# A four-layer trunk on one core: another order at the beginning, and the log/exp table loaded explicitly after the lower bounds

## The chip, the cores and the metric

The kernel runs on 1 core of one Trainium2 chip. The metric is the time of one execution in device microseconds. The kernel before took 3142.55 us, the median of 3 runs (3138.03 to 3144.14).

## The reference, cut to what matters

Four layers (HGRN2, RWKV-7, MLA, HGRN2) work on 256 context tokens and 256 latent tokens of 1024 channels. Each layer begins with a norm that is shifted and scaled by a modulation made from `c` and `c_ctx`. Only the beginning and the first HGRN2 layer matter here:

```python
silu_c = jax.nn.silu(c); silu_cc = jax.nn.silu(c_ctx)
mod_l = jnp.split((silu_c @ w_mod[layer] + b_mod[layer])[:, None, :], 6, axis=-1)
h_l = modulate(rmsnorm(x_l, norm1[layer]), mod_l[0], mod_l[1])
# lower bounds, from hg_lb alone
lb_p = jnp.cumsum(jax.nn.softmax(hg_lb, axis=1), axis=1); lower_bounds = lb_p - lb_p[:, :1]
# hgrn2_mixer, 8 heads of 128
q, i, g, z_f, z_b = jnp.split(h @ w_in, 5, axis=-1)
gates = jnp.log(lb + (1.0 - lb) * jax.nn.sigmoid(z)), (1.0 - lb) * jax.nn.sigmoid(-z)
b = jnp.cumsum(gc, axis=-2)     # per chunk of 64; then exp(b), exp(b - b_mid), exp(b_end - b)
o = rmsnorm(o, g_norm) * jax.nn.silu(g) @ w_o
```

## The kernel before, in words

All 512 tokens (256 of the context, 256 latent) lie transposed in SBUF, as eight tiles `xT` of 128 channels by 512 tokens. A product in float32 is made of three matmuls of split operands (`hh`/`hl` and `whi`/`wlo`): a weight tile `wraw` is cast on ScalarE (`whi`, line 432), its rest is taken on VectorE (`wlo`, 433), and both have three buffers.

`start` (342) is the beginning, called by `hgrn` for layer 0 (750). `load_x` (330) loads `x` and `ctx` through SyncE's queue and turns them over on TensorE (339). `params` (282) loads all small parameters as rows of 128 into seven staging tiles and turns each over into `prm` (323, 324). The first tile holds `c`, `c_ctx`, `norm1`, the bias `b_mod` of layer 0 and `norm2`; `hg_lb` lies in the third. The tiles are buffers of the same ring of 16 (`mraw`) that the modulation's weights use. `silu_c` (354) makes the operand `sc` of the modulation: a memset on GpSimd, then two Silu on ScalarE. `lower_bounds` (696) makes a softmax over two rows with two Exp. `mod` (384) runs over 3 groups of 32 weight tiles of 256 KB (397, 398); the first group is needed before the first projection, the other two are laid between the projections.

Then `norm_mod` (528) squares `xT` on ScalarE (509), adds on GpSimd and VectorE (513), sums with TensorE (518) and takes the root by Ln and Exp (491, 492). After that come 8 heads, one after another. A head has four projections (24 matmuls each, lines 457 to 459) and a scan. In `hgrn`, sigmoid, its logarithm and silu are made of Exp, Ln and Exp (724, 725, 731, 810), the decays of Exp (908, 916 to 930). VectorE multiplies (932 to 934), TensorE turns the result over (`tr`, 938), ScalarE copies it back (940). So Ln and Exp follow each other several times in each head.

A ScalarE function needs its table on the engine, and a load is an instruction of its own (ACT_TABLE_LOAD), put in by the compiler where the function isn't in the table that is there. `table` (498) loads by hand one table that has both Ln and Exp. It is called by `norm_mod` (531) and `leave` (633). The order of the instructions on each engine is made by a scheduler that lays them out by its own estimate of their times; the table loads that the compiler puts in aren't in the source.

Of the kernel before, what the change touches and what calls it, by code (L numbers as in the profile page):

```python
# [122 lines left out]
class Jobs:  # L123
# [20 lines left out]
    def schedule(self, places, stage, lat, ordered, locks=(), eps=0.05):  # L144
# [48 lines left out]
        while len(order) < len(self.list):  # L193
            best = (math.inf,)
            for x in ready:
                t = start(x, best[0])
                if t is not None:
                    best = min(best, (math.floor(t / eps), x.place, x.index, t))
            x, t = self.list[best[2]], best[3]
            for y in x.takes:  # L200
                r = y["ring"]
                if r == ordered:
                    todo[int(x.pair)] -= 1
                if len(live[r]) >= self.rings[r]:
                    old = [i for i, o in enumerate(live[r]) if not o["left"]]
                    live[r][min(old, key=lambda i: live[r][i]["end"])] = y
                else:
                    live[r].append(y)
            end = ended(x, t) if x.engine == "PE" else t + x.cost
            free[x.engine] = end  # L210
            if x.engine == "Pool":
                port[0] = max(port[0], end)
            ready.remove(x)
            order.append(x)
            for y in x.takes + x.uses:
                y["left"] -= 1
                y["end"] = max(y["end"], end + x.lag)
            for y in x.then:
                y.at = max(y.at, end + x.lag + lat[x.engine, y.engine])
                y.need -= 1  # L220
                if not y.need:
                    ready.append(y)
# [3 lines left out]
class Trunk:  # L226
# [55 lines left out]
    def params(self, raw, psum):  # L282
        nc, a = self.nc, self.a
        rows = []

        def add(name, ap):
            rows.append((name, ap, ap.shape[0]))

        def flat(t):
            names = "abcd"[: len(t.shape)]  # L290
            f = t.rearrange(f"{' '.join(names)} -> ({' '.join(names)})") if len(t.shape) > 1 else t
            return f.rearrange("(r p) -> r p", p=P)

        add("c", flat(a["c"]))
        add("c_ctx", flat(a["c_ctx"]))
        add("norm1", flat(a["norm1"]))
        add("b_mod0", flat(a["b_mod"][0]))
        add("norm2", flat(a["norm2"]))
        for l in range(1, DEPTH):
            add(f"b_mod{l}", flat(a["b_mod"][l]))  # L300
        for n in ("hg_lb", "hg_norm", "ffn_conv", "ffn_conv_b", "rw_mu", "rw_w0", "rw_a0", "rw_k_k", "rw_k_a",
                  "rw_r_k", "rw_ln_w", "rw_ln_b", "mla_q_norm", "mla_kv_norm", "norm_f"):
            add(n, flat(a[n]))
        total = sum(r for _, _, r in rows)
        ntile = -(-total // P)
        self.prm = self.cst.tile([P, ntile * P], F32, name="prm")
        self.off = {}
        stage = [raw()[:, :P] for i in range(ntile)]
        if total % P:
            nc.vector.memset(stage[-1], 0.0)  # L310
        pos = 0
        for name, ap, r in rows:
            self.off[name] = pos
            done = 0
            while done < r:
                t, o = divmod(pos, P)
                n = min(P - o, r - done)
                nc.scalar.dma_start(out=stage[t][o:o + n, :], in_=ap[done:done + n, :])
                done += n
                pos += n  # L320
        for i in range(ntile):
            ps = psum()
            nc.tensor.transpose(ps[:, :P], stage[i], self.ident)
            nc.vector.tensor_copy(self.prm[:, i * P:(i + 1) * P], ps[:, :P])

    def col(self, name, i=0, n=1):
        o = self.off[name] + i
        return self.prm[:, o:o + n]
# [12 lines left out]

    def start(self, l, raw, xs, psum1, psum2):

        self.load_x(xs, psum2)
        self.params(raw, psum2)
        self.silu_c()
        self.lower_bounds()
        steps = self.mod(l, raw, psum1)
        for _ in range(5):
            next(steps)  # L350
        yield
        yield from steps

# [101 lines left out]
    def mm3(self, ps, wh, wl, xh, xl, start, stop):  # L455
        nc = self.nc
        nc.tensor.matmul(ps, lhsT=wh, rhs=xh, start=start, stop=False)  # L457
        nc.tensor.matmul(ps, lhsT=wh, rhs=xl, start=False, stop=False)  # L458
        nc.tensor.matmul(ps, lhsT=wl, rhs=xh, start=False, stop=stop)  # L459
# [2008 lines left out]
```

## Time and profile before

| | |
|---|---|
| median of 3 runs | 3142.55 us |
| profiled execution | 3137.63 us |
| its span | 3135.9 us |
| TensorE (PE) busy in the span | 2877.7 us, 92% |
| ScalarE (ACT) busy in the span | 1396.8 us, 45% |
| mean granted TensorE clock | 0.942 |

Busy time adds up an engine's instructions. A matmul's end is modelled, so a busy PE isn't a PE at its peak. Idle time of an engine that isn't the bottleneck costs nothing. In a timeline, the bracket at a row's end gives how long the engine sat idle before it and what released it.

### The profile page before, as it was taken

The numbers are of one execution on the slowest core, as the hardware profiler recorded it, in microseconds if no ns is written. First come the engines' busy times: TensorE is split into PE (matmuls) and PEld (weight loads), VectorE is DVE, ScalarE is ACT, GpSimd is POOL, SyncE is SP. The second block draws the span as 40 slices with busy tenths as digits, with TensorE's granted clock in tenths as the row PEclk, the third lists the DMA queues.
The fourth block names the chain that finished last, engine by engine and source line by source line (L and its number), as shares of the span: only waits on it lengthen the run. The fifth ranks groups of instructions, "written<-read, shape, count | busy, mean of one in ns | idle before, by whom it ended". The sixth has DMA issues, their size and how long they took to land.

```text
span 3135.9 us, 53648 instructions
## 1 busy us (share of the span) xinstructions
PE 2877.7 (92%) x21377; PEld 2314.6 (74%) x21377; DVE 1777.8 (57%) x3163; ACT 1396.8 (45%) x2668; POOL 525.8 (17%) x706
## 2 busy tenths in 40 slices
PE   7999989999787777888879999999899999999899
PEld 4588877778666555666658888866688888888898
DVE  4277765445673356867554434566454344488765
ACT  3266544334442145565543223345343233577544
POOL 1023222222342133434310000000000000133000
PEclk9999989999888888888779999999999999999999
DMA  7622168886756865666552232201133322332454
GB/s 277 198 68 68 58 232 270 280 287 217 232 180 198 229 197 157 173 170 193 162 164 94 94 101 88 80 31 34 39 103 101 94 94 68 94 95 82 155 183 133
DMA packets 475276, 452.77 MB, mean 144 GB/s; under 512 B 98428, under 2 KB 415762, under 8 KB 474898
## 3 DMA queue, kind: packets, MB, share of 16 engines
q1 hardware_dynamic: 458288, 398.27, 41.0%
q0 software_dynamic: 15360, 50.34, 4.7%
q8 instruction: 168, 2.75, 0.4%
q10 hardware_dynamic: 1378, 0.73, 0.1%
q14 instruction: 82, 0.67, 0.1%
HBM read 392.64 MB, written 56.10 MB: 143 GB/s over the span
## 4 chain that ended last, share of the span: by engine, by line
PE 80%; DVE 8%; DMA 5%; ACT 4%; issue 2%; SPq 1%; POOL 1%; ACTq 0%; DVEq 0%; POOLq 0%
PE mm L457 20%; PE mm L458 19%; PE mm L459 19%; DMA mraw<-in_w_mod_dram 2%; PE sc L2247 1%; PE at L398 1%; PE md L2091 1%; PE o L2279 1%; PE at L1025 1%; PE ax L1543 1%; DMA vw<-prev 1%; PE ax L398 1%; DVE t L1125 1%; PE pt L2266 1%; DVE itmp L1636 1%
## 5 line engine op out<-in xcount | busy, mean ns | idle before, releaser
L457 PE MATMUL mm<-hh,whi 128*128 128x512 f32 (+1 forms) x2088 | 751.7, 367 | 18.7 <-ACT hh L622 8.5
L458 PE MATMUL mm<-hl,whi 128*128 128x512 f32 (+1 forms) x2088 | 756.3, 363 | 4.0 <-DVE hl L553 3.3
L459 PE MATMUL mm<-hh,wlo 128*128 128x512 f32 (+1 forms) x2088 | 752.7, 362 | 1.0 <-DVE wlo L433 1.0
L433 DVE TENSOR_TENSOR wlo<-wraw,whi 128x1024 fp32r<-128x1024 f32 (+1 forms) x388 | 463.2, 1195 | 413.8 <-ACT whi L432 397.5
L432 ACT CAST whi<-wraw 128x1024 fp32r<-128x1024 f32 (+1 forms) x388 | 395.2, 1020 | 546.9 <-PE mm L458 492.6
L457 PEld LDWEIGHTS mm<-hh,whi 128*128 128x128 f32 x2088 | 396.5, 192 | 97.1 <-issue 11.9
L458 PEld LDWEIGHTS mm<-hl,whi 128*128 128x128 f32 x2088 | 400.7, 192 | 68.3 <-issue 6.9
L459 PEld LDWEIGHTS mm<-hh,wlo 128*128 128x128 f32 x2088 | 399.8, 192 | 65.5 <-issue 5.9
L457 PE MATMUL mm<-uh,whi 128*128 128x512 f32 (+1 forms) x764 | 266.1, 349 | 0.0
L458 PE MATMUL mm<-ul,whi 128*128 128x512 f32 (+1 forms) x764 | 265.7, 348 | 0.0
L459 PE MATMUL mm<-uh,wlo 128*128 128x512 f32 (+1 forms) x764 | 264.9, 348 | 0.0
L277 POOL MEMSET reset<- 128x512 f32 x3 | 1.6, 526 | 1019.7 <-DVE xn L621 1019.6
L457 PEld LDWEIGHTS mm<-uh,whi 128*128 128x128 f32 x764 | 144.5, 189 | 21.8 <-ACT phi L449 1.7
L458 PEld LDWEIGHTS mm<-ul,whi 128*128 128x128 f32 x764 | 144.6, 189 | 18.1
L459 PEld LDWEIGHTS mm<-uh,wlo 128*128 128x128 f32 x764 | 144.2, 189 | 18.3
L450 DVE TENSOR_TENSOR plo<-praw,phi 128x512 fp32r<-128x512 f32 x64 | 44.2, 691 | 158.1 <-ACT phi L449 158.0
L449 ACT CAST phi<-praw 128x512 fp32r<-128x512 f32 x64 | 39.6, 619 | 198.7 <-DMA praw<-in_rw_w_rkv_dram 122.9
L2341 DVE SCALAR_TENSOR_TENSOR t<-mm,prm,t 128x510 f32<-128x510 f32 (+1 forms) x88 | 60.0, 682 | 101.8 <-ACT t L2339 101.8
L2339 ACT ACTIVATE t<-mm,prm 128x512 f32<-128x512 f32 (+1 forms) x88 | 63.1, 718 | 105.5 <-PE mm L459 105.3
L914 POOL TENSOR_TENSOR t<-t 128x512 f32<-128x512 f32 x32 | 44.5, 1392 | 359.2 <-DVE t L904 233.4
L2091 PE MATMUL md<-mraw,sc 128*32 128x256 f32 x768 | 73.5, 451 | 31.3 <-DMA mraw<-in_w_mod_dram 29.3
L2348 DVE TENSOR_TENSOR t<-t,mm 128x512 f32<-128x512 f32 (+1 forms) x88 | 53.7, 619 | 57.7 <-PE mm L459 57.4
(476 smaller groups left out, 5301.8 us busy)
## 6 DMA issues: line engine op xcount, KB each, us to landing
wraw<-in_ffn_w_in_dram SPq DMA_DIRECT2D x176, 512.0 KB, 3.6
mraw<-in_w_mod_dram SPq DMA_DIRECT2D x192, 256.0 KB, 5.7
mraw<-in_w_mod_dram SPq DMA_DIRECT2D x96, 512.0 KB, 5.3
wraw<-in_hg_w_in_dram SPq DMA_DIRECT2D x80, 512.0 KB, 3.8
wraw<-in_ffn_w_out_dram SPq DMA_DIRECT2D x80, 512.0 KB, 3.3
ow<-preo SPq DMA_DIRECT2D x64, 256.0 KB, 4.1
praw<-in_rw_w_rkv_dram POOLq DMA_DIRECT2D x48, 256.0 KB, 4.5
vw<-prev SPq DMA_DIRECT2D x32, 256.0 KB, 4.6
```

The costliest lines, as they stand in the source:

```text
L398: nc.tensor.matmul(ps[32 * i:32 * i + 32, :], lhsT=self.sc[:, k, :], rhs=t, start=(k == 0), stop=(k == KT - 1), tile_position=(0, 32 * i))
L432: nc.scalar.copy(h, r)
L433: nc.vector.tensor_tensor(out=w, in0=r, in1=h.bitcast(F32), op=ALU.subtract)
L450: nc.vector.tensor_tensor(out=lo, in0=raw, in1=hi.bitcast(F32), op=ALU.subtract)
L457: nc.tensor.matmul(ps, lhsT=wh, rhs=xh, start=start, stop=False)
L458: nc.tensor.matmul(ps, lhsT=wh, rhs=xl, start=False, stop=False)
L459: nc.tensor.matmul(ps, lhsT=wl, rhs=xh, start=False, stop=stop)
L914: nc.gpsimd.tensor_tensor(out=c3(de), in0=b3[:, :, end:end + 1].to_broadcast([P, 8, 64]), in1=b3, op=ALU.subtract)
L2091: nc.tensor.matmul(g["ps"][32 * c:32 * c + 32, halves[f]], lhsT=self.sc[:, k, :], rhs=g["raw", u][:, c], start=k == 0 and f == 0, stop=k = ...
L2339: nc.scalar.activation(c[:, sl], pa[b][:, sl], AF.Identity, bias=self.prm[:, cb + j + b:cb + j + b + 1], scale=w[1])
L2341: nc.vector.scalar_tensor_tensor(out=c3[:, :, 1:], in0=p3[:, :, :255], scalar=w[0], in1=c3[:, :, 1:], op0=ALU.mult, op1=ALU.add)
L2348: nc.vector.tensor_tensor(out=ss[b][:, sl], in0=ss[b][:, sl], in1=pv[b][:, sl], op=ALU.mult)
```

## The change

The first parameter tile is still loaded from ScalarE's queue; the other tiles' loads (23) are issued by GpSimd. The first tile is turned over and silu is asked for ahead of `load_x`. The other tiles and the lower bounds come after the first five steps of the modulation in the source. Behind the lower bounds, `start` calls `table`. Lines of the changed file are higher than before: by 6 behind `start`.

```diff
@@ params
-                nc.scalar.dma_start(out=stage[t][o:o + n, :], in_=ap[done:done + n, :])
+                (nc.gpsimd if t else nc.scalar).dma_start(out=stage[t][o:o + n, :], in_=ap[done:done + n, :])
...
             nc.vector.tensor_copy(self.prm[:, i * P:(i + 1) * P], ps[:, :P])
+            if not i:
+                yield
@@ start
-        self.load_x(xs, psum2)
-        self.params(raw, psum2)
+        rows = self.params(raw, psum2)
+        next(rows)
         self.silu_c()
-        self.lower_bounds()
+        self.load_x(xs, psum2)
         steps = self.mod(l, raw, psum1)
         for _ in range(5):
             next(steps)
+        for _ in rows:
+            pass
+        self.lower_bounds()
+        self.table()
         yield
         yield from steps
```

The scheduler makes of this another order on every engine. ScalarE at the beginning, before (`sc` is silu's result, `lbt` belongs to the lower bounds, the table load at 359 is Silu's, that at 709 Exp's):

```order
L318 DMA mraw<-in_norm_f_dram 8x128
L359 ACT_TABLE_LOAD
L359 ACTIVATE sc<-prm 128x8 x2
L709 ACT_TABLE_LOAD
L709 ACTIVATE lbt<-lbt 128x16
L710 ACTIVATE lbt<-lbt 128x16
L509 ACTIVATE t_364<-xT_81 128x512
```

And now (505 is the explicit load in `table`, 365 Silu's load, 497 and 498 are Ln and Exp of the first norm):

```order
L438 CAST whi<-wraw 128x1024
L515 ACTIVATE t_384<-xT_88 128x512
L438 CAST whi<-wraw 128x1024 x2
L715 ACTIVATE lbt<-lbt 128x16
L716 ACTIVATE lbt<-lbt 128x16
L505 ACT_TABLE_LOAD
L365 ACT_TABLE_LOAD
L365 ACTIVATE sc<-prm 128x8 x2
L497 ACT_TABLE_LOAD
L497 ACTIVATE rs_399<-rs_398 128x4
L498 ACT_TABLE_LOAD
L498 ACTIVATE rs_399<-rs_399 128x4
```

Silu now stands behind the squares of the norm, three weight casts and the lower bounds' two Exp. Before, the explicit load (499) stood behind the first norm's Exp. Now the one explicit load of the beginning stands directly ahead of Silu's, which replaces it, and there is no other until the end of the layer's mixer.

ScalarE in the fifth of the first layer's eight heads, before (`rs` is the norm of a head's output, `tr` the turned product, `mm` the projections):

```order
L491 ACTIVATE rs_2448<-rs_2447 128x4
L492 ACTIVATE rs_2448<-rs_2448 128x4
L940 COPY t_2303<-tr 128x512
L724 ACTIVATE t_2497<-mm 128x512
L724 ACTIVATE t_2533<-mm 128x512
L725 ACTIVATE t_2497<-t_2497 128x512
L725 ACTIVATE t_2533<-t_2533 128x512
L731 ACTIVATE t_2497<-t_2497 128x512
```

And now, the same instructions:

```order
L497 ACT_TABLE_LOAD
L497 ACTIVATE rs_2449<-rs_2448 128x4
L498 ACT_TABLE_LOAD
L498 ACTIVATE rs_2449<-rs_2449 128x4
L946 COPY t_2304<-tr 128x512
L730 ACTIVATE t_2498<-mm 128x512
L730 ACTIVATE t_2534<-mm 128x512
L731 ACT_TABLE_LOAD
L731 ACTIVATE t_2498<-t_2498 128x512
L731 ACTIVATE t_2534<-t_2534 128x512
L737 ACT_TABLE_LOAD
L737 ACTIVATE t_2498<-t_2498 128x512
```

Between one norm's Ln and the next there are now eight loads in such a head, where there was none: ahead of 497, 498, 731, 737, 731, 816, 731 and 922. In the whole program ScalarE's order has 102 loads now and had 36. From the second or third head on, the other engines' orders in this layer's mixer are as before.

GpSimd at the beginning, now (the memset of `sc` followed the masks directly before):

```order
L318 DMA mraw<-in_rw_ln_b_dram 8x128
L318 DMA mraw<-in_mla_q_norm_dram 2x128
L318 DMA mraw<-in_mla_kv_norm_dram 2x128
L318 DMA mraw<-in_norm_f_dram 8x128
L363 MEMSET sc 128x256
L519 TENSOR_TENSOR t_365<-t_365,t_367 128x512
```

The memset that silu waits for stands behind all 23 issues.

## Rows read from the trace of the kernel before

**Rows 1.** Stretches: PE, PEld, DVE, ACT, POOL busy (count), granted PE clock, DMA share, GB/s.

```profile
20.00:47.50 27.50, 19.80 (x98) 6.95 (x98) 10.08 (x23) 15.03 (x23) 4.15 (x3) 0.81 0.95 334
98.00:163.00 65.00, 65.00 (x251) 28.92 (x250) 18.89 (x24) 18.68 (x30) 7.55 (x8) 1.00 0.61 204
280.00:320.00 40.00, 40.00 (x315) 33.80 (x314) 29.18 (x49) 26.23 (x52) 12.39 (x13) 1.00 0.23 67
```

**Rows 2.** Timeline of the beginning: start, us, engine, line, instruction, [idle before, releaser].

```profile
3.11 0.31 POOL L357 MEMSET sc<- 128x256 f32 x1
13.83 24.94 SPq L397 DMA_DIRECT2D mraw<-in_w_mod_dram  x32
23.70 1.28 ACT L359 ACT_TABLE_LOAD   x1 [23.70 <-DMA mraw<-in_w_mod_dram]
25.00 0.31 ACT L359 ACTIVATE sc<-prm 128x8 f32<-128x8 f32 x2
48.57 0.50 PE L786 MATMUL mm<-whi,hh 128*128 128x512 f32 x1 [1.76 <-ACT hh L552]
```

**Rows 3.** What SyncE's queue waited for until 48 us: us, times, longest.

```profile
SPq L397 <- DMA mraw<-in_b_mod_dram: 5.6, 1, 5.6
```

**Rows 4.** Timeline of GpSimd at 394 us: one DMA that it issues.

```profile
394.01 0.54 POOL L448 DMA_DIRECT2D praw<-in_rw_w_rkv_dram  x1
```

**Rows 5.** Timeline of ScalarE: a table load between two dependent instructions.

```profile
41.30 0.20 ACT L491 ACTIVATE rs<-rs 128x4 f32<-128x4 f32 x1 [6.07 <-DVE rs L490]
41.52 1.28 ACT L492 ACT_TABLE_LOAD   x1
42.81 0.20 ACT L492 ACTIVATE rs<-rs 128x4 f32<-128x4 f32 x1
```

**Rows 6.** Timeline of ScalarE in the fifth head.

```profile
284.45 0.20 ACT L491 ACTIVATE rs<-rs 128x4 f32<-128x4 f32 x1 [2.06 <-DVE rs L490]
...
285.64 0.59 ACT L940 COPY t<-tr 128x512 f32<-128x512 f32 x1 [0.75 <-PE tr L938]
...
296.65 1.05 ACT L432 CAST whi<-wraw 128x1024 fp32r<-128x1024 f32 x1 [2.64 <-PE mm L458]
...
298.77 0.62 ACT L916 ACTIVATE t<-t 128x512 f32<-128x512 f32 x1
...
300.85 0.62 ACT L930 ACTIVATE t<-t 128x512 f32<-128x512 f32 x1
303.53 1.05 ACT L432 CAST whi<-wraw 128x1024 fp32r<-128x1024 f32 x1 [2.06 <-PE mm L458]
306.44 0.58 ACT L940 COPY t<-tr 128x512 f32<-128x512 f32 x1 [1.86 <-PE tr L938]
...
307.78 0.69 ACT L883 ACTIVATE rd<-at,prm 128x512 f32<-128x512 f32 x1 [0.56 <-PE at L1025]
...
311.69 1.06 ACT L432 CAST whi<-wraw 128x1024 fp32r<-128x1024 f32 x1 [0.65 <-PE mm L458]
314.57 0.21 ACT L491 ACTIVATE rs<-rs 128x4 f32<-128x4 f32 x1 [1.83 <-DVE rs L490]
```

**Rows 7.** Timeline of VectorE in the fifth head.

```profile
301.57 0.92 DVE L932 TENSOR_TENSOR kx<-t,t 128x256 f32<-128x256 f32 x1
...
303.30 0.96 DVE L934 TENSOR_TENSOR t<-kx,pe 128x256 f32<-128x256 f32 x1
```

**Rows 8.** Timeline of TensorE in the fifth head.

```profile
305.81 0.60 PE L938 MATMUL tr<-ident,t 128*128 128x128 f32 x4
```

**Rows 9.** Timeline of TensorE in the last layer: a wait between matmuls.

```profile
2643.55 0.79 PE L771 MATMUL mm<-whi,hh 128*128 128x256 f32 x2 [3.94 <-ACT whi L432]
```

**Rows 10.** Stretches about that wait, TensorE alone: busy, granted clock, DMA share, GB/s.

```profile
2642.00:2644.00 2.00, 0.45 (x2) 0.50 0.00 0
2644.00:2646.00 2.00, 1.53 (x7) 0.50 0.08 10
2646.00:2648.00 2.00, 2.00 (x12) 0.50 0.87 269
```

More of the change, by code (lines that the diff above doesn't have):

```diff
@@ L342, in start @@
     def start(self, l, raw, xs, psum1, psum2):
+        rows = self.params(raw, psum2)
+        next(rows)
+        self.silu_c()
         self.load_x(xs, psum2)
-        self.params(raw, psum2)
-        self.silu_c()
-        self.lower_bounds()
         steps = self.mod(l, raw, psum1)
```

## The prediction

> **What bounds the kernel now.** I read the stretches first, since the change touches only the beginning and, through the table loads, the first layer's mixer. Until 47.5 us the core is bound by loading: 334 GB/s while TensorE is busy for 19.80 of 27.50 us [rows 1]. Then TensorE is busy without a gap, 65.00 of 65.00 us with the first head and 40.00 of 40.00 with the fifth, at full clock [rows 1]. ScalarE's busy time there, 26.23 of 40 us, looks like much room [rows 1]. Then I read the timelines: of the beginning, for who gates the first modulation matmul, and of one head, for where ScalarE's free time lies and who waits behind it.
>
> **The beginning.** Before, silu ran at 25.00, behind its table load at 23.70, since ScalarE first had to issue all 28 parameter loads [rows 2]. The modulation's weights were issued from 13.83 on, 32 loads in 24.94 us, after SyncE's queue had waited 5.6 us for one small parameter load [rows 2, 3]. Now the small loads leave both queues, and the weights follow the four loads of `x` directly. But silu isn't early. On ScalarE it stands behind three weight casts, and those weights (0.52 MB each) are issued behind nine of the modulation's tiles (0.26 MB each). Up to the third cast some 2.1 + 10 x 0.26 + 3 x 0.52 = 6.3 MB must have come, at 334 GB/s 19 us, so near 20.5 us from the first issue on; then a cast (1.05 [rows 6]), two Exp of 0.2, two table loads of 1.28 [rows 5]: about 24.5. GpSimd's memset for silu was at 3.11 and now follows 23 issues; at 0.54 us each [rows 4] that is 12.4 us, done near 16 if it never waits for a landing. So silu comes at 24 to 25, as before, and more of the weights is there by then. Counting bytes, 32 modulation tiles, six weight tiles and `x` are 13.6 MB, 41 us at 334 GB/s; before, the 32nd issue was at 38.77 and the first projection at 48.57 [rows 2]. I estimate 4 us won. The bounds: 8 won, if loading never pauses, and 8 lost, if each of GpSimd's issues takes twice 0.54 us by waiting for the landing of earlier ones, so that silu comes near 32.
>
> **The table loads.** The explicit load is now replaced at once by Silu's, so the layer's Ln and Exp each ask for a table of their own: 66 loads more. One takes 1.28 us, and nothing runs beside it on ScalarE: the Ln ends at 41.50, the load is at 41.52, the Exp at 42.81 [rows 5]. So 1.30 us each, and 1.4 where the two instructions overlapped by 0.1 before. Fewer than ten lie ahead of 163 us, where ScalarE is busy for 18.68 of 65 us [rows 1]: these I cost at nothing, covered by the projections.
>
> The Trainium skill, page "ScalarE: Activation LUTs", section "What ACT_TABLE_LOAD costs", gives 1.28 us for the load and 1.38 us of drain, 2.66 us for every switch. Of that the trace agrees with the load; of the drain it shows nothing, since 0.02 us lie between the Ln's end and the load and 0.01 us behind it [rows 5]. By the page the eight switches of a head would take 21.3 us, by the rows 10.4; I go by the rows.
>
> In a head, ScalarE is idle for 0.75 + 2.64 + 2.06 + 1.86 + 0.56 + 0.65 + 1.83 = 10.35 us of 30.12 (284.45 to 314.57) [rows 6]. Eight loads want 10.4 to 10.8. The sum of the room is thus just used up, and what counts is where it lies. I walk the head with ScalarE's lateness. The first Ln's load lies in the 2.06 us ahead of it: 0. The Exp's load makes 1.3; the gap of 0.75 ahead of the copy leaves 0.55. Then come four loads with no gap between them (731, 737, 731, 816): 0.55 + 4 x 1.35 = 5.95. The gap of 2.64 ahead of the cast at 296.65 leaves 3.3. Two loads more (731, 922) make 6.0 at the instruction that was at 298.77, and the one at 300.85 is as late: it ends at 307.5 in place of 301.47 [rows 6].
>
> VectorE took it up at 301.57 and was through with the three products at 304.26 [rows 7]; now 307.55 and 310.2. TensorE turns the last one over at 305.81 [rows 8], and it takes its instructions in order, with projections queued behind the transposes: it waits from 305.81 to 310.2, **4.4 us**. From there on everything that ScalarE does hangs on TensorE again: of the remaining 6.0 us of lateness TensorE's own shift takes 4.4, and the gaps of 2.06 and 1.86 the rest [rows 6]. The next head starts without lateness. So it is 4.4 us in each head. The casts are late by up to 6 us too, but they are made for the third buffer, two projections of some 6 us ahead; those I cost at nothing. If that cover fails, TensorE waits there in place of, not beside, the transposes.
>
> The first head's chain lies in the stretch before 163 us; seven are left: 7 x 4.4 = 30.8 us. The bounds: 0, if the loads find room that I don't see, and 66 x 1.28 = 84.5, if each lies on the path.
>
> **The clock after such a wait.** Where TensorE waited 3.94 us between matmuls (2639.6 to 2643.55) [rows 9], the granted clock had fallen to 0.5 (1.2 in place of 2.4 GHz) before the wait was over, and 0.45 + 1.53 + 2.00 us of work behind it ran at that level [rows 10]. Half of those 3.98 us is lost: 2.0 us. The bounds are 0 and 2.0 for each wait. The waits in the heads are slightly longer than that one, so I lie near it, and let the clock fall in four of five: 1.6, and 7 x 1.6 = 11.2 us.
>
> **The sum.** 30.8 + 11.2 - 4 = +38.0 us on the profiled execution's 3137.63: 3175.6. The median of the runs shown lies 4.9 us above that execution, so I say **3180 us**.
>
> **The rivals.**
> 1. Not slower: the loads vanish in ScalarE's idle time. The sums stand for it (10.35 us of room, 10.4 wanted), and it holds if the product that TensorE turns over at 305.81 had 6 us to spare. It has 1.55 (304.26 to 305.81) [rows 7, 8]. Then only the beginning counts: 3142.55 - 4 = 3138.5, or 3134.5 at the bound. Chance 0.08.
> 2. The beginning is late: GpSimd's 23 issues wait for landings, silu comes near 32, and the first projection with it: +8 in place of -4, so 3192. For it: the memset that silu needs stands behind all of them. Against: the loads are small. Chance 0.12.
> 3. The clock doesn't fall in the waits, or hardly: 30.8 - 4 = +26.8, 3169. Against it stand [rows 9, 10]. Chance 0.2.
> 4. Every load is seen in full, since TensorE also waits for accumulators that ScalarE empties late: +84.5 - 4, 3223. Against it: seven heads give ScalarE 10 us of idle time each, and four of the eight loads lie in it. Chance 0.06.
> 5. A switch costs twice what it does in [rows 5], where ScalarE had little in flight ahead of it. Then the eight in a head take 8 x 2.6 = 20.8 us beside 19.8 of work, 40.6 for a head that has 30.1: at least 7 x 10.5 - 4 = +69.5, 3212. Chance 0.04; the 0.02 us ahead of the load speak against it. This is about what the price of the Trainium skill's page "ScalarE: Activation LUTs", section "What ACT_TABLE_LOAD costs", makes of it: 8 x 2.66 + 19.8 = 41.1 us a head.
>
> My forecast has 0.5. Faster by over 0.2% (6.3 us; about what a measurement of this kernel can tell from no change) needs rival 1 and more than 6 us from the beginning: 0.03. Within 0.2%: 0.05. Slower: 0.92. The range reaches down to half of the waits without a fall of the clock (30.8 / 2 - 4 = +11.4, 3154) and up to a late beginning with a fall in every wait (7 x 6.4 + 8 = +52.8, 3195) and somewhat into rival 5; I set 3155 to 3203.
>
> **What would show it.** Right: 102 table loads on ScalarE, at 1.28 us, 8 of them in each of the middle heads; heads that follow each other at 34 to 37 us in place of 30.1; in front of each head's first transposes (now line 944) a wait of TensorE of about 4 us that VectorE's product (940) ends, with a fall of the granted clock in some; ScalarE busy for over 30 us of a head; first projection near 44 to 45 us; from the feed-forward part of layer 0 on nothing but a shift. Wrong: heads still at 30 us, loads longer than 1.3 us, TensorE waiting for weights (wlo) and not for the product, or a first projection behind 50 us.

## The result, and the profile after

The changed kernel takes 3178.03 us, the median of 4 runs (3167.65 to 3184.51), against 3140.29 for the kernel before in the same session (4 runs, 3135.47 to 3144.14). The ratio is 1.012, with a 95% interval of 1.0095 to 1.0144: **slower by some 38 us, as forecast (3180, 3155 to 3203)**. The profiled execution, the fastest of the four, took 3167.65 us; its span is 3165.9 us, 30.0 more than before. All ratios here are taken over all the runs and differ a little from the quotient of the two medians.

First the stretches of the beginning, the first head with its projections, and the fifth head (columns as in [rows 1]):

```profile
20.00:47.50 27.50, 19.80 (x94) 6.94 (x94) 9.06 (x22) 9.01 (x14) 5.60 (x9) 0.76 0.94 320
98.00:163.00 65.00, 65.00 (x324) 34.88 (x323) 21.98 (x30) 30.54 (x43) 7.55 (x8) 1.00 0.61 194
280.00:320.00 40.00, 36.82 (x283) 31.16 (x282) 26.10 (x43) 34.27 (x54) 10.23 (x12) 0.96 0.22 62
```

From 280 to 320 us TensorE was busy for 40.00 us at full clock before [rows 1]; now it is 36.82, at 0.96, and ScalarE has gone from 26.23 to 34.27. From 98 to 163 us, with six of the added loads, TensorE is still busy without a gap. The first projection starts at 50.15 us (48.57 before [rows 2]).

What TensorE waited for between 160 and 440 us (us in total, times, longest); before, the heads had one wait of 0.2 us. One of the two waits at 531 (0.8 us) lies behind the last head's transposes:

```profile
PE tr L944 <- DVE t L940: 21.6, 8, 3.9
PE mm L463 <- DVE t L815: 2.2, 1, 2.2
PE rd L531 <- DVE rs L501: 1.6, 2, 0.8
PE mm L463 <- DVE g L738: 1.2, 1, 1.2
```

The wait stands where the prediction put it: in front of the transposes (938, now 944), for VectorE's product (934, now 940). Here is ScalarE's way into one of them, on its timeline (start, us, engine, line, instruction, [idle before, releaser]):

```profile
316.15 0.60 ACT L730 ACTIVATE g<-mm 128x512 f32<-128x512 f32 x1
316.78 1.28 ACT L731 ACT_TABLE_LOAD   x1
...
318.72 1.28 ACT L922 ACT_TABLE_LOAD   x1
...
322.11 0.61 ACT L936 ACTIVATE t<-t 128x512 f32<-128x512 f32 x1
322.63 1.03 ACT L438 CAST whi<-wraw 128x1024 fp32r<-128x1024 f32 x1
326.33 0.59 ACT L946 COPY t<-tr 128x512 f32<-128x512 f32 x1 [2.67 <-PE tr L944]
```

The gap of 2.64 us ahead of the cast [rows 6] is gone, two loads stand where nothing stood, and behind the last Exp (936) and one cast ScalarE is idle for 2.67 us, since now it waits for TensorE. On TensorE's timeline the same place, and then the 5 us behind it as a stretch:

```profile
325.20 1.09 PE L944 MATMUL tr<-ident,t 128*128 128x128 f32 x4 [3.88 <-DVE t L940]
```

```profile
325.20:330.20 5.00, 5.00 (x20) 4.71 (x21) 4.33 (x5) 2.11 (x5) 1.45 (x1) 0.50 0.39 108
```

After 3.88 us of waiting the granted clock is 0.50 for 5 us (and 1.00 in the 5 us behind them), and four transposes take 1.09 us in place of 0.60 [rows 8].

### The profile page after: what moved, and what is told of

Read it like the earlier page. It is cut to its first block, busy times and chain, and to the rows that moved or that the text cites. A ratio compares the mean times of both kernels' runs of the same rounds, so it can differ in the third digit from the quotient of the medians.

```text
span 3165.9 us, 53752 instructions
## 1 busy us (share of the span) xinstructions
PE 2874.7 (91%) x21377; PEld 2318.6 (73%) x21377; DVE 1780.1 (56%) x3163; ACT 1484.2 (47%) x2734; POOL 530.9 (17%) x729
## 4 chain that ended last, share of the span: by engine, by line
PE 72%; DVE 9%; ACT 8%; DMA 5%; issue 4%; POOL 1%; SPq 1%; DVEq 0%; ACTq 0%; POOLq 0%
PE mm L463 17%; PE mm L464 17%; PE mm L465 17%; DMA mraw<-in_w_mod_dram 1%; PE sc L2253 1%; PE at L404 1%; PE md L2097 1%; PE o L2285 1%; DMA vw<-prev 1%; ACT whi L438 1%; PE ax L1549 1%; ACT L731 1%; DVE t L1131 1%; PE ax L404 1%; PE pt L2272 1%
```

## The experiments

A yardstick for all: the time from the first modulation copy (line 401 before; [rows 2] show the beginning it ends) to the eighth head's second transposes, the last of the first mixer (the expectations of 9 to 11 say "first transposes", but their numbers are this yardstick's). It leaves out the beginning and everything behind the first mixer. In the kernel before it is 374.30 - 45.52 = 328.78 us, in the changed one 404.32 - 47.10 = 357.22: +28.4, of the 30.0 in the span. Where TensorE doesn't wait, profiles agree in it within hundredths (experiments 2 to 4), while whole runs of one kernel spread over 7 to 27 us. Behind each median stand 4 to 12 runs of a kernel and 7 to 29 of the kernel before in the same session.

**1. The explicit load taken out of the changed kernel.**

```diff
         self.lower_bounds()
-        self.table()
         yield
```

> The changed kernel without the explicit table load in start(). Its built order still has 102 table loads on ScalarE, and the load that the first layer's norm asks for by itself stands at the same place, directly ahead of Silu's load. Theory (the log/exp table is lost since lower_bounds is now recorded behind the first modulation steps, so that the norm's own load is pinned behind lower_bounds' Exp and Silu's load follows it; the explicit line has no effect of its own): 3178 us, within 6 us of the changed kernel, heads still 35 to 38 us apart. Rival (the explicit load is what drives the table out): 36 loads, about 3134 us.

3174.8 us against 3148.0, ratio 1.0107 (1.0084 to 1.013); yardstick 400.87 - 46.34 = 354.53. The loss stays. The load that `norm_mod` asks for by itself stands at the same place in the built order, between lower_bounds' Exp and Silu's load. What moved it there is the new order of the recording: a load made by hand stays behind the ScalarE instruction recorded last, which was the first modulation copy before and is lower_bounds' Exp now. Then Silu, which the scheduler lays behind that Exp, replaces it. The explicit line makes no difference that these runs show. That the place of lower_bounds alone would do it, without the rest of the change, is read from the order; no run moved it by itself.

**2. The explicit load one line lower.**

```diff
         self.lower_bounds()
-        self.table()
         yield
+        self.table()
         yield from steps
```

> The changed kernel with the explicit load one line lower, behind the yield: it is then recorded behind the modulation's steps and comes to stand behind Silu, ahead of the heads; the built order has 37 loads. Everything else of the change stays. Theory (the 66 loads cost about 36 us in the heads; the beginning costs 1.6 us and the bunched modulation matmuls give back 7.6): heads back at 30.1 to 30.7 us, TensorE's clock at 1.00 from 200 us on, 3132 to 3137 us, about 6 below the kernel before. Rival (part of the loss comes from the late beginning or from the other queue, not from the loads): 3145 us or more.

3141.88 us against 3148.0, ratio 0.998 (0.9965 to 0.9995), 6 below the kernel before as expected, though its beginning was late (first modulation copy at 51.53); yardstick 372.61 - 51.53 = 321.08. The heads are back at 30.1 and 30.7 us from the third on, the clock is 1.00 from 200 us to the end of the heads. The explicit load stands at 104.97 us, behind the last copy of `it` (796) and ahead of the first head. The stretch of the fifth head:

```profile
280.00:320.00 40.00, 40.00 (x327) 33.87 (x326) 29.31 (x49) 26.65 (x53) 10.79 (x11) 1.00 0.23 67
```

On TensorE the built order of this kernel and of experiment 1 is the same instruction for instruction, and on ScalarE it differs by the loads alone; the changed kernel's is the same too. So their difference, 354.53 - 321.08 = 33.4 us (36.1 for the changed kernel), is what the 66 loads cost.

**3. The explicit load alone, in the kernel before.**

```diff
         self.lower_bounds()
+        self.table()
```

> The kernel before with nothing but the explicit load behind lower_bounds. The built order has 35 loads: the two loads ahead of the first norm's Ln and Exp are gone, one stands behind lower_bounds. Theory: the heads stay at 30.1 us; the first projection comes up to 2.6 us earlier (two loads of 1.28 us on the chain of the first norm), so 3138 us. Rival (an explicit load as such loses the table): 102 loads' worth, 3175 us or more. Rival (that chain is hidden behind the weights' loading): 3140 us, no change.

3147.03 us against 3148.0, ratio 1.0006 (0.9992 to 1.002); yardstick 373.10 - 44.32 = 328.78, the same as before to the last digit. The two loads of the first norm are gone (its Ln and Exp follow each other at 39.50 and 39.74 us), and the first projection comes at 47.37 us in place of 48.57, but the median shows no gain.

**4. The queue alone, in the kernel before.**

```diff
-                nc.scalar.dma_start(out=stage[t][o:o + n, :], ...)
+                (nc.gpsimd if t else nc.scalar).dma_start(out=stage[t][o:o + n, :], ...)
```

> The kernel before with nothing but the parameter tiles after the first issued from GpSimd's queue; the recording order of before stays, so the norm's load stands behind the first modulation copy and the built order has 36 loads. Its modulation matmuls already stand in the order of the changed kernel (19 alone, against 26 before). Theory (the gain of 7.6 us between 98 and 160 us comes from fewer modulation matmuls that stand alone, and that from the queue): 3133 to 3136 us, first projection at 49 to 50 us. Rival (the gain came with the first tile's early use): 3140 us or more.

3140.07 against 3148.0 us, ratio 0.9987 (0.997 to 1.0003), so not told from no change in the median. The yardstick is clear: 366.95 - 45.88 = 321.07, the 321.08 of experiment 2. The 7.7 us that the change gains between the first modulation copy and the heads come with the queue, since the scheduler then lays fewer modulation matmuls singly between the projections.

**5 and 6. Four loads more in each head, at two places of the kernel before.**

```diff
+    for _ in range(2):
+        self.table("exp_and_others")
+        self.table()
```

In 5 this stands behind the Exp of line 930 (first direction), in 6 between the gate's Ln and second Exp.

> The kernel before with two pairs of table loads more in each of the first layer's eight heads (another set and the log/exp set back, twice: 4 x 1.28 = 5.1 us), in the built order behind the Exp of line 930, where ScalarE was idle for 2.06 us ahead of a weight cast and 1.86 us ahead of the copy of line 943 (940 before). Theory (what counts is where the loads lie): the 3.9 us take most of it; 0 to 8 us more than the kernel before, heads at 30.1 to 31 us, no wait of TensorE for the product. Rival (each load is seen in full): 32 x 1.28 = +41 us. Rival (only the sum of the idle time in a head counts, 10.35 us against 5.1): 0.

3147.91 against 3147.13 us, ratio 1.000 (0.9983 to 1.0017); heads 30.3 to 30.6 us apart (one 32.6, which was 32.7 before), no wait of TensorE in them. The yardstick is 376.89 - 45.01 = 331.88, +3.1. So 32 loads, 41 us of ScalarE's time, cost 3 us, and none of it as a wait for the product: they aren't seen in full. Whether their place or their sum (5.1 us a head) spares the rest, this run doesn't tell; 8 does. TensorE's order hardly moved: from the third to the seventh head its transposes stand within 2 instructions of their old places.

> The kernel before with the same two pairs of loads in each of the eight heads, but ahead of the gate's second Exp (line 734). In the built order they stand directly ahead of the Exp of line 920 in the second, fourth and sixth head, in the run without a gap that leads to the product; in the other heads they stand behind the Exps, ahead of idle time. Theory (where they lie counts): in those three heads TensorE waits 5.1 - 1.55 = 3.6 us at the transposes and loses 1 to 2 us more by the clock, in the others at most 1 us; +14 to +20 us in all, and spacing from head to head alternates. Rival (the sum of the idle time counts): 0, as with the loads in the room. Rival (each load in full): +41 us, the same in every head.

3156.69 us, ratio 1.0029 (1.0018 to 1.0041); yardstick 380.03 - 45.40 = 334.63, +5.9. The heads alternate (39.0, 22.4, 40.0, 22.4 us), but the wait I had expected isn't there. What TensorE waited for:

```profile
PE mm L457 <- DVE t L812: 4.6, 4, 1.5
```

Neither number came: not 14 to 20, not 0. The reason is in the built order. A load that is written out is an instruction that the scheduler sees, and it moved TensorE's transposes: in the third and fourth head they are the 836th and 974th matmul in place of the 813th and 996th. So this run alone can't tell the theories apart.

**7. As many loads as the changed kernel has, written out: a pair ahead of each of a head's four Ln.**

```diff
+        if self.pairs:
+            self.table("exp_and_others")
+            self.table()
         nc.scalar.activation(l[:, sl], l[:, sl], AF.Ln, bias=1.0)
```

> The kernel before with eight table loads more in each of the first layer's eight heads (two, another set and the log/exp set back, ahead of each of the four Ln), the number that the changed kernel has in a head, but written out in the code, so that the scheduler reckons with them when it orders the other engines. Theory (the changed kernel loses its time since the order of TensorE was made without the 66 loads, and the product comes late for a fixed place; 10.2 us of loads would fit beside 19.8 us of work into 30.1): no wait at the transposes, heads at 30.1 to 32 us, 0 to 14 us more than the kernel before. Rival (ScalarE is simply full with eight loads more): heads at 35 to 37 us, +36 us as in the changed kernel.

3193.6 us, ratio 1.0139 (1.0116 to 1.0162); yardstick 422.22 - 44.03 = 378.19, +49.4. My theory fell: that the order knew of the loads did not help. But ScalarE isn't simply full either. It was idle for 3.77 us in front of one copy (945), waiting for TensorE, and TensorE waited for ScalarE at a new place:

```profile
PE at L1030 <- ACT am L1006: 27.8, 7, 4.2
```

```profile
273.47 0.59 ACT L945 COPY t<-tr 128x512 f32<-128x512 f32 x1 [3.77 <-PE tr L943]
273.96 0.60 ACT L724 ACTIVATE t<-mm 128x512 f32<-128x512 f32 x1
274.58 2.57 ACT L499 ACT_TABLE_LOAD   x2
...
277.77 2.57 ACT L499 ACT_TABLE_LOAD   x2
```

Four loads stand close together, and the copies `am` that TensorE needs next come behind them. So each of the two engines waits for the other in turn. Of the 49.4 us the waits at 1030 are 27.8; from the third head on the granted clock is 0.91 over each head, in place of 1.00.

**8. Loads that the scheduler does not see, in the run without a gap.**

```diff
+        if t2[0] == "g" and self.hgj == 0:
+            for f in (AF.Silu, AF.Sigmoid, AF.Silu):
+                e = self.sm.tile([P, 8], F32, tag="other", name="other")
+                self.tc.keep_in_program_order(nc.scalar.activation(e, l[:, 256:264], f))
+            self.table()
         nc.scalar.activation(l[:, sl], l[:, sl], AF.Exp, scale=-1.0)
```

> The kernel before with, in each of the first layer's eight heads, three tiny activations (128x8) of other table sets between the gate's Ln and its second Exp, and an explicit load of the log/exp set behind them. In the built order that makes five loads in a middle head, most of them ahead of the Exp of line 936 (930 before) on which the product for the transposes rests; four of the five are put in after the engines' order is made, and TensorE's transposes stand within 2 instructions of their old places. 5 x 1.28 + 3 x 0.2 = 7.0 us of ScalarE's time in a head that has 10.35 us of idle time. Theory (where the loads lie counts, in an order that doesn't reckon with them): the product is 7.0 - 0.5 (an Exp that now stands behind) - 1.55 = 4.9 us late where all five stand ahead of it, 2 where three do; TensorE waits there, 3 to 5 us a head, and loses 1 to 2.5 by the clock; +25 to +45 us. Rival (the sum of the idle time counts, as the four loads in the room cost nothing): 0 to +5 us, no wait at the transposes.

3182.9 against 3143.6 us, ratio 1.0127 (1.0107 to 1.0148): +39 us; yardstick 417.94 - 44.08 = 373.86, +45.1. Heads are 35.0 to 41.5 us apart from the second on. What TensorE waited for, and ScalarE's timeline in one head:

```profile
PE tr L944 <- DVE t L940: 25.7, 7, 5.8
```

```profile
247.05 0.62 ACT L922 ACTIVATE t<-t 128x512 f32<-128x512 f32 x1
247.69 1.28 ACT L734 ACT_TABLE_LOAD   x1
...
249.21 1.28 ACT L734 ACT_TABLE_LOAD   x1
...
250.73 1.28 ACT L924 ACT_TABLE_LOAD   x1
...
252.67 1.28 ACT L734 ACT_TABLE_LOAD   x1
...
254.19 1.28 ACT L499 ACT_TABLE_LOAD   x1
255.49 0.63 ACT L926 ACTIVATE t<-t 128x512 f32<-128x512 f32 x1
256.02 0.61 ACT L936 ACTIVATE t<-t 128x512 f32<-128x512 f32 x1
```

Seven us in a head that has 10.35 us of idle time [rows 6] cost at least as much as the changed kernel's eight loads, since in five heads all of them stand ahead of the Exp at 936: there TensorE waits 4.0 to 5.8 us (4.9 expected). In the one head where three of the five stand ahead of that Exp it waits 2.2 us (2 expected). In 5, 5.1 us behind that Exp cost 3 us in all eight heads together. That is the walk of the prediction, shown: where the loads lie counts, not whether their sum fits.

**9 to 11. Modulation matmuls in bunches.** Load 8 (or 16) weight tiles, then record their matmuls, the last loaded first, so that none can start early:

```diff
-                    nc.tensor.matmul(ps[32 * i:32 * i + 32, :], lhsT=self.sc[:, k, :], rhs=t, ...)
+                    held.append((t, k, i))
+                if len(held) < bunch:
+                    continue
+                for t, q, i in sorted(held, key=lambda u: (-u[1], u[2])):
+                    nc.tensor.matmul(ps[32 * i:32 * i + 32, :], lhsT=self.sc[:, q, :], rhs=t, ...)
+                held.clear()
```

In the kernel of experiment 2 by 16 (9), then by 8 (10), and in the kernel before by 8 alone (11):

> The changed kernel with the explicit load behind the yield, and the first layer's modulation matmuls recorded in bunches: 16 weight tiles are loaded, then the 16 matmuls that use them are recorded, the last loaded first. In the built order 8 stand alone (19 in the changed kernel, 26 before). Theory (a modulation matmul alone between projections costs 1.1 us more than one in a bunch: 7.70 us for 7 fewer): from the first modulation copy to the last head's first transposes 321.1 - 12 = 309 us, median about 0.994 of the kernel before. Rival (the 7.70 us came from something else in the order, or the bunches wait for their last tile and hold up the weights queued behind): 321 us or more.

3148.51 us against 3147.13, ratio 1.0011 (0.9999 to 1.0023); yardstick 373.38 - 53.05 = 320.33. The rival's number came for 16, near enough: TensorE waits at the first group's bunch for its last tile (at 45.3 us, ahead of the yardstick), and inside the yardstick, at 63.0 us, for the norm's `hl`.

```profile
PE at L409 <- DMA mraw<-in_w_mod_dram: 4.3, 1, 4.3
PE at L409 <- DVE hl L565: 4.0, 1, 4.0
```

> As the bunches of 16, but of 8: in the built order 11 modulation matmuls stand alone. Theory (1.1 us for each alone): 321.1 - 9 = 312 us from the first modulation copy to the last head's first transposes, median about 0.995 of the kernel before. Rival (the bunches wait for loading): 321 us or more; smaller bunches then lose less than those of 16.

3133.89 us, ratio 0.9959 (0.9947 to 0.9971): **faster than both kernels**. The yardstick is 365.14 - 47.18 = 317.96, 3.1 us less than in experiment 2, not 9: the price of 1.1 us for each lone matmul was too high (below).

> The kernel before with nothing but the modulation matmuls recorded in bunches of 8: in the built order 10 stand alone (26 before, 19 with the queue alone, 11 with bunches of 8 in the changed kernel). Theory (the gain behind the first modulation copy is a matter of the matmuls' order, wherever it comes from): 317 to 321 us from the first modulation copy to the last head's first transposes, against 328.8 before and 318.0 with the bunches in the changed kernel. Rival (it needs the parameter loads off ScalarE's queue): 326 us or more.

3137.24 against 3146.86 us, ratio 0.9965 (0.9952 to 0.9978); yardstick 363.92 - 45.77 = 318.15. So the order of these matmuls is worth 10.6 us of the kernel before, and that needs nothing else of the change.

**12. Bunches of 8, the load behind the yield, and one more load behind silu.**

```diff
         self.silu_c()
+        self.table()
```

> The changed kernel with the explicit load behind the yield and bunches of 8, and a further explicit load behind silu: in the built order the first norm's Ln and Exp need no load any more (36 loads). Theory (the two loads of 1.28 us stand on the first norm's chain): 1 to 2.6 us less at the first projection than with the bunches of 8 alone, 3130 to 3134 us where the kernel before has 3140 to 3147, ratio about 0.995. Rival (the weights' loading hides them, as the explicit load alone showed no gain in the median): the same as with the bunches of 8, ratio 0.996.

3137.48 against 3146.86 us, ratio 0.9967 (0.9953 to 0.998), yardstick 364.53 - 46.51 = 318.02: the same as 11 (0.9965), and as 10, which is this kernel without that load (0.9959), within the intervals. The rival holds. The first projection starts at 49.61 us against 50.26.

## Why the prediction was right, point by point

**The 66 loads: right.** There are 102, 8 in each middle head. ScalarE's busy time rose by 87.4 us (1396.8 to 1484.2), 1.32 for each, with the load itself at 1.28, and a load starts within 0.03 us of the end of the instruction ahead of it (316.75 and 316.78 above). The rival of the doubled price falls with it. By the Trainium skill's 2.66 us for a switch (page "ScalarE: Activation LUTs", section "What ACT_TABLE_LOAD costs") it would have been 176, an estimate from that page's price; the trace agrees with the page's load, not with its drain.

**Why they come: right in effect, wrong in name.** "The explicit load is now replaced at once by Silu's" is what the order shows, but without the explicit load it is the same (experiment 1). It comes from the recording order, by which the norm's own load stands behind lower_bounds' Exp and Silu behind that load. Neither the explicit load (3) nor the queue (4) does it by itself.

**The wait: right in place, too long in sum.** Forecast 7 x 4.4 = 30.8 us. Up to the last head's second transposes TensorE's waits in the heads add up to 25.8 us, against 0.8 in experiment 2 with the same order: 25.0 us. The walk itself held, in the head for which it was made. The ends of that walk, before and then now (TensorE's second transposes of the head ahead, then VectorE's last product):

```profile
285.01 0.60 PE L938 MATMUL tr<-ident,t 128*128 128x128 f32 x4
```

```profile
300.38 0.60 PE L944 MATMUL tr<-ident,t 128*128 128x128 f32 x4
324.23 0.83 DVE L940 TENSOR_TENSOR t<-kx,pe 128x256 f32<-128x256 f32 x1
```

The last Exp started 15.84 us behind those transposes before (300.85 [rows 6]) and starts 21.73 behind them now (322.11): 5.9 us late, 6.0 in the walk. VectorE's three products then take 2.2 us in place of 2.7, and so the wait is 3.88 and not 4.4. What failed is the factor of seven: one head stood for all. At the first transposes the later heads wait 1.8, 2.5, 3.8, 3.2, 3.9, 3.2 and 2.0 us, 20.3 in all. Heads follow each other at 35.1 to 38.5 us (34 to 37 forecast), with ScalarE busy for 29.9 us of a middle head (over 30 forecast). The other 5.5 us are waits about the first two heads and ahead of the eighth (463, 531 and one head's second transposes) that the walk didn't have.

**The clock: right.** Forecast 7 x 1.6 = 11.2 us, with a fall in four of five waits. In five of seven heads the first 10 us from the transposes on show a granted clock of 0.83, 0.72, 0.85, 0.75 and 0.86; in the other two, behind waits of 1.77 and 1.99 us, it stayed at 1.00. TensorE is busy throughout these stretches, so what is missing to 1.00 is lost: 9.9 us. The two longest falls cost 2.8 and 2.5 us, more than the bound of 2.0 for one wait. Waits and clock make 34.9 of the 36.1 us; the rest stays open.

**The beginning: wrong.** Forecast -4 us, measured +1.6, and the first projection came at 50.15 us, not at 44 to 45: by the prediction's own list (behind 50 us) a sign of being wrong. What failed is the estimate from bytes at 334 GB/s: it doesn't have the waits that SyncE's queue makes for itself. The trace, first ScalarE, then one wait of SyncE's queue between 12 and 28 us (us, times, longest), then VectorE:

```profile
22.39 1.04 ACT L438 CAST whi<-wraw 128x1024 fp32r<-128x1024 f32 x1 [0.43 <-DMA wraw<-in_hg_w_in_dram]
24.41 0.21 ACT L715 ACTIVATE lbt<-lbt 128x16 f32<-128x16 f32 x1 [0.97 <-DVE lbt L713]
...
24.74 1.28 ACT L505 ACT_TABLE_LOAD   x1
26.03 1.28 ACT L365 ACT_TABLE_LOAD   x1
27.33 0.31 ACT L365 ACTIVATE sc<-prm 128x8 f32<-128x8 f32 x2
47.10 0.59 ACT L407 COPY modev<-at 128x512 f32<-128x512 f32 x1 [3.87 <-PE at L404]
```

```profile
SPq L437 <- DVE lbt L718: 3.5, 1, 3.5
```

```profile
24.58 2.18 DVE L439 TENSOR_TENSOR wlo<-wraw,whi 128x1024 fp32r<-128x1024 f32 x1
```

The third cast came at 22.39 in place of 20.5, behind weights that were later than counted, and then VectorE's part of the lower bounds took another 0.97 us. Silu is at 27.33, 2.3 us later than before [rows 2], and the first modulation copy 1.6 later. GpSimd's memset wasn't what held it: it ran at 18.98, later than the 16 reckoned but ahead of the casts' end, so the second rival fell. The tiles were not there earlier either. SyncE's queue had issued 14 of the 32 by 22.7 us, and the next only at 27.47. In between it stood at weight loads (437). A weight tile has three buffers, and the fourth, fifth and sixth weight load went out at 21.77, 23.25 and 26.79, each 0.03 us behind the end of VectorE's rest (439) of the first, second and third weight (21.74, 23.22 and 26.76). The profile names 718 for the last of these waits, an instruction of VectorE that starts only at 26.88. Before, the fourth weight load was issued behind all 32 modulation tiles, at 38.86; now weight loads stand among them and hold up the tiles behind. But the beginning is not good to 2 us: the changed kernel and experiments 1 and 2, alike up to there, have that copy at 47.10, 46.34 and 51.53 us.

**A gain that I had not seen: -7.7 us.** I costed the stretch from 98 to 163 us at nothing. The change of queues alone makes the scheduler lay the modulation's other 64 matmuls in another order: 19 alone between projections in place of 26. On the timeline of TensorE in the kernel before, two of those:

```profile
133.71 1.05 PE L398 MATMUL at<-mraw,sc 128*32 128x512 f32 x2
134.69 0.49 PE L457 MATMUL mm<-hh,whi 128*128 128x512 f32 x1
135.12 1.05 PE L398 MATMUL at<-mraw,sc 128*32 128x512 f32 x2
```

And a bunch, in the kernel of experiment 4:

```profile
98.60 3.64 PE L398 MATMUL at<-mraw,sc 128*32 128x512 f32 x32
```

One instruction here is two records. Alone it takes 0.97 to 0.98 us to the next start, and the projection's matmul behind it 0.34 to 0.43 in place of 0.23; in this bunch each takes 3.64 / 16 = 0.23. That is about 0.9 us for each that joins such a bunch, 6 us for seven. By line, the matmuls' busy time from 44 to 200 us (busy us, mean ns | idle before), in the kernel before and in experiment 4:

```profile
L398 PE MATMUL at<-mraw,sc 128*32 128x512 f32 x136 | 37.1, 600 | 0.0
```

```profile
L398 PE MATMUL at<-mraw,sc 128*32 128x512 f32 x136 | 31.9, 600 | 0.3 <-DVE mod L373 0.3
```

5.2 us of the 7.7. Another 1.1 are waits of TensorE inside the yardstick (3.4 before, 2.3 then), and 0.9 are the projections' matmuls behind a lone one; the last 0.5 stays open. Going on from 19 alone to 11 brought only 3.1 us: the 64 matmuls' time from start to next start, added up from the timeline without waits, was 34.2 us before, 28.7 with 19 alone and 26.9 with 11. The length of a bunch tells why. Five of them, in experiment 10:

```profile
113.29 1.90 PE L409 MATMUL at<-mraw,sc 128*32 128x512 f32 x10
```

To the next start, one takes 0.98 us and two together 0.98 too; four take 1.07, five 1.83, six 1.91, sixteen 3.57. So the time goes by begun fours, some 0.9 us each (the code gives four in a row the four column positions of `tile_position`). In begun fours the 64 matmuls are 35 before, 30 with 19 alone and 28 with 11 alone. The expectations' 1.1 us for each lone matmul were wrong for that reason: a bunch of five costs two fours.

**The sum: met by luck.** On the profiled pair it is +1.6 - 7.7 + 36.1 = +30.0, against +38.0 forecast: 25.0 of waits for 30.8, 9.9 of clock (with 1.2 that stays open) for 11.2, +1.6 at the beginning for -4, and the -7.7 that wasn't in the sum. The medians are 37.7 apart, but the profiled execution is the fastest of the four, and experiment 1, with the same orders, has a ratio of 1.0107 in place of 1.012. Behind the first mixer both profiles need the same 2761.6 us, by chance: in the other profiles it is up to 2782, most of the scatter between 700 and 1800 us; experiments 1 and 2, alike in TensorE's order, need 2780.3 and 2770.0. So the cause and its place were forecast; that 3180 was met to 2 us is luck, with terms that were off by 1 to 8 us each and a scatter of some 10 us on either side.

**Not slower**, the rival on the other side, fell as argued: the product had 1.55 us to spare, and the loads in front of it more than that.

## What to carry to other kernels

An engine with idle time has room only where it is idle ahead of a deadline: find the last instruction in its run that another engine, in its fixed order, waits for, and count what is added in front of that; the sum over the period says little. Table loads that a compiler puts in are in nobody's plan: after each change of the recording order, count them, and place the one that unites the functions where a later instruction cannot take it out. A count of bytes is a bound only while the queue moves: look for loads in it that wait for a buffer. And look at how small matmuls are strewn between large ones: here bunches of eight were worth 0.35% (0.22 to 0.48) without any other change.

## What the runs showed of the hardware that was not expected

A matmul of 32 columns by 512 that stands alone between full ones takes 0.98 us and makes the next one 0.1 to 0.2 us longer; two or four in a row take hardly more than one (0.98 and 1.07), and in a bunch of 16 each takes 0.23. Two table loads in a row take 2.57 us, so here nothing is paid for a switch but the load. The fall of the clock after a wait is not the same each time. In the changed kernel a wait of 3.88 us was followed by 5 us at 0.50 (above), which cost 2.5 us; in experiment 1 the same wait, in the same head and also of 3.88 us, was followed by none:

```profile
323.21:328.21 5.00, 5.00 (x30) 4.44 (x31) 4.94 (x6) 3.43 (x8) 1.90 (x2) 1.00 0.37 107
```

That is part of why two runs of one order differ: 36.1 us lost in the heads in the one, 33.4 in the other, with 9.9 and 7.5 of them by the clock.
